# A hybrid decoder block on one core: the framework's scheduler orders all engines with its finer model of the machine

## The chip, the core and the metric

One core of a Trainium2 chip. The time is device microseconds of one execution, the median of several runs. The core's engines run side by side, each its own list of instructions in order: TensorE (PE, with its weight loads PEld), VectorE (DVE), ScalarE (ACT), GpSimd (POOL), and SyncE (SP), which issues most DMAs. Semaphores tie the lists together.

## The reference

x is 2048 x 1024 in f32, one layer.

```python
mod = cs @ ada_w + ada_b                        # sh1, sc1, g1, sh2, sc2, g2
h = rmsnorm(x, norm1_g) * (1 + sc1) + sh1
p = h @ w_in                                    # 3456 columns, shared out among three mixers
ya = rglru_mixer(...)                           # 256 wide: conv, gates, a linear scan over time
yb = hgrn2_mixer(...)                           # 384 wide: 6 heads, gated linear attention
yc = rwkv7_mixer(...)                           # 384 wide: 6 heads, a delta rule with state S per head
x = x + g1 * ((concat[ya, yb, yc] * mix_beta) @ w_out)
h = rmsnorm(x, norm2_g) * (1 + sc2) + sh2
x = x + g2 * ((silu(h @ w_gate) * (h @ w_up)) @ w_down)     # 2816 wide
out = rmsnorm(x, final_g)
```

rwkv7_mixer steps through time with `S = S * w + sa (kk a)^T + v k^T`, `y = S r`; the kernel does this in chunks of 64 steps.

## The kernel before

Time is cut into four blocks b = 0 to 3 of 512 columns, features lie on the 128 partitions.

*Dense products.* All of w_in, w_out, w_gate, w_up, w_down go through `project`. Each f32 operand is split into a high part in fp32r (ACT, line 78, `wh` or `hh`) and the remainder (DVE, line 221, `wl` or `hl`), and each 128 x 128 by 128 x 512 product is three matmuls at line 248, which add up in a PSUM bank `pd` (three of these):

```python
for n, (a, b) in enumerate(((wh, hh), (wh, hl), (wl, hh)), 3 * k):
    PE.matmul(p, a[:, c], b, start=(n == 0), stop=(n == tot - 1))
```

There are 9696 of them: 2592 for w_in, then per block 192 for w_out, 1056 up and 528 down, 1776 in all. A weight piece of 128 x 512 serves 12 matmuls per block; it is loaded by SP into one of three `wr` and split into one of four `wh`/`wl`.

*Mixers.* `mixers(b)` runs rwkv on three pairs of heads, hgrn on three pairs and rglru on two, on what w_in left in DRAM (`pd` there), and writes y to DRAM (`yd`). rwkv uses tiles `tr` and banks `pm`, `pc`; hgrn and rglru use `th` and the one bank `ph`. One rwkv pair goes so: low-rank projections (PE lines 488, 489), gates, a scan and decays (tables of ACT change several times), KG and BK (DVE 529 to 542), products within chunks (PE 553) masked on DVE (556, 557), transposes (562), the upper 32 x 32 blocks to DRAM (`nd`) and back over all partitions (`NL`, `NX`), a substitution of 30 x 2 short DVE operations (599, 601), back over DRAM (`xd`), transposes and two products (617 to 627), then the recurrence: eight chunks, each a chain PE 641, 642 - DVE 644 and ACT `rs` - PE 650 - DVE 651 and ACT `VS` - PE 653, 654 - DVE `VS` at line 81, and the next chunk begins from that state. A norm (257, 258: block sums), a gate (669) and the store end it. The three pairs of a block share tiles and follow one another, and the state ties block to block.

*What ties mixers and dense work.* w_out of block b needs all of its y: `load_y(b)` reads back `yd`, k = 0 to 7, where k = 5 to 7 are rwkv's pairs.

```python
def mixers(b):
    with level("mix"):
        lr = lora(b)
        rwkv(b, 0, lr); hgrn(b, 0); rglru(b, 0)
        rwkv(b, 1, lr); rwkv(b, 2, lr)
        hgrn(b, 1); rglru(b, 1); hgrn(b, 2)
...
    for b in range(NB):
        if b + 1 < NB:
            mixers(b + 1)
        with level("feed"):
            ys, before = ffn(b, *w_out_products(b, ys, before))
```

(Several lines of `mixers` stand on one here.)

*What sets the order.* The framework's scheduler takes the instructions as the program issues them, keeps a model of the machine running, and gives each engine, when the model says it can take one, the ready instruction with the lowest number. The numbers come from `level`:

```python
clock = {"out": -1000000, "load": 0, "feed": 1000000, "mix": 2000000, "dense": 3000000}
```

So mixers go before dense matmuls wherever the model has them ready. The lists that come out are fixed when the kernel is built.

## Time and profile before

| | |
|---|---|
| median of 3 runs | 2881.95 us (2878.94 to 2886.17) |
| the profiled execution | 2884.81 us |
| its span, first to last instruction | 2883.0 us |
| mean granted TensorE clock | 0.986 |
| instructions | 41762 |

In the profile's groups a line reads: line, engine, operation, output <- inputs, shapes, count | busy us, mean ns of one | idle time of the engine before them and what ended it. An f32 matmul of the mixers is recorded as two. Windows give, for each stretch, its length and the busy time of PE, PEld, DVE, ACT and POOL with counts, then granted clock, DMA share and GB/s.

### The profile page before, as it was taken

To read this page: it belongs to the slowest core of one execution; us is meant where nothing else is said; L and a number is where in the kernel's file an instruction comes from. 1 tells how busy PE (TensorE), PEld (TensorE's weight loads), DVE (VectorE), ACT (ScalarE), POOL (GpSimd) and SP (SyncE) were. 2 spreads that over 40 slices of the span, in tenths; PEclk is the share of its full clock that TensorE was granted. 3 is DMA by queue.
4 is the path that set the end of the run, shared out by engine and by line. 5 is a ranking of instruction groups with operands and counts; after the bars stand their busy time and mean duration, and the time that the engine had idled before them with its cause. 6 is when DMAs were issued, how large, how long until landed. Compare 5 with 4: busy or idle time off the path is not lost. (4 is left out here: it accounts for less than half of the span.)

```text
span 2883.0 us, 41762 instructions
## 1 busy us (share of the span) xinstructions
PE 2761.2 (96%) x14842; PEld 2189.4 (76%) x14842; DVE 1975.3 (69%) x4617; ACT 1500.2 (52%) x2514; POOL 81.5 (3%) x67
## 2 busy tenths in 40 slices
PE   7999999999999899999989999999999999999998
PEld 6777777777777677777767787777777888788886
DVE  8776768778586777868788777778964444644445
ACT  4528465263636737565684556757644233533323
POOL 2000000000001000000100000001000001000000
PEclk9999999999999999999999999999999999999999
DMA  7534455434344233333453233344432333433332
GB/s 255 161 103 142 137 160 182 129 121 133 98 125 142 89 88 100 103 92 100 115 160 88 84 105 101 96 114 122 122 94 88 96 99 117 146 99 96 98 96 87
DMA packets 235041, 337.52 MB, mean 117 GB/s; under 512 B 73041, under 2 KB 78673, under 8 KB 234833
## 3 DMA queue, kind: packets, MB, share of 16 engines
q1 hardware_dynamic: 160144, 285.55, 31.9%
q10 hardware_dynamic: 74688, 49.31, 6.7%
q8 instruction: 117, 1.92, 0.3%
q14 instruction: 92, 0.75, 0.1%
HBM read 286.53 MB, written 48.23 MB: 116 GB/s over the span
## 5 line engine op out<-in xcount | busy, mean ns | idle before, releaser
L248 PE MATMUL pd<-hh,wh 128*128 128x512 f32 x3232 | 1285.4, 399 | 16.6 <-ACT hh L78 14.2
L248 PE MATMUL pd<-hl,wh 128*128 128x512 f32 x3232 | 1289.3, 399 | 3.1 <-DVE hl L81 3.0
L248 PE MATMUL pd<-hh,wl 128*128 128x512 f32 x3232 | 1283.6, 397 | 0.0
L78 ACT ACTIVATE wh<-wr 128x512 fp32r<-128x512 f32 (+1 forms) x752 | 463.6, 620 | 865.3 <-PE pd L248 713.4
L221 DVE TENSOR_TENSOR wl<-wr,wh 128x512 fp32r<-128x512 f32 (+1 forms) x752 | 509.0, 681 | 315.6 <-ACT wh L78 307.7
L248 PEld LDWEIGHTS pd<-hh,wh 128*128 128x128 f32 x3232 | 611.3, 189 | 144.0 <-ACT hh L78 17.7
L248 PEld LDWEIGHTS pd<-hl,wh 128*128 128x128 f32 x3232 | 611.8, 189 | 129.1 <-DVE hl L81 7.4
L248 PEld LDWEIGHTS pd<-hh,wl 128*128 128x128 f32 x3232 | 611.9, 189 | 121.9 <-issue 2.6
L81 DVE SCALAR_TENSOR_TENSOR xs<-pd,Q,xs 128x512 f32<-128x512 f32 x224 | 167.6, 748 | 124.6 <-PE pd L248 114.5
L78 ACT ACT_TABLE_LOAD x183 | 234.8, 1283 | 12.1 <-issue 4.7
L78 ACT ACTIVATE xs<-pd 128x512 f32<-128x512 f32 x140 | 82.8, 591 | 66.0 <-PE pd L248 60.8
L78 ACT ACTIVATE th<-th 128x512 f32<-128x512 f32 (+2 forms) x153 | 93.7, 613 | 44.9 <-DVE th L787 19.7
L917 DVE TENSOR_TENSOR xs<-pd,xs 128x512 f32<-128x512 f32 x88 | 60.7, 690 | 77.0 <-PE pd L248 75.2
L78 ACT ACTIVATE hh<-xs 128x512 fp32r<-128x512 f32 x120 | 74.1, 627 | 38.1 <-DVE xs L917 25.3
L78 ACT ACTIVATE hw<-VS,we 64x64 f32<-64x64 f32 x192 | 66.0, 344 | 42.2 <-DVE VS L81 38.8
L599 DVE TENSOR_TENSOR ftmp<-NX,NL 128x30 f32<-128x30 f32 (+4 forms) x360 | 73.9, 205 | 8.6 <-issue 1.2
L601 DVE TENSOR_TENSOR NX<-NX,ftmp 128x30 f32<-128x30 f32 (+4 forms) x360 | 73.7, 205 | 7.2
L78 ACT ACTIVATE tr<-tr 128x512 f32<-128x512 f32 (+3 forms) x100 | 62.3, 626 | 16.8 <-DVE tr L81 15.0
L81 DVE SCALAR_TENSOR_TENSOR VS<-pc,we,hw 64x64 f32<-64x64 f32 x168 | 47.4, 282 | 32.7 <-PE pc L653 28.9
L217 POOL TENSOR_TENSOR hl<-xs,hh 128x512 fp32r<-128x512 f32 x32 | 46.8, 1488 | 810.4 <-ACT hh L78 571.3
L78 ACT ACTIVATE xs<-xs 128x512 f32<-128x512 f32 x77 | 47.7, 626 | 36.1 <-DVE xs L81 22.9
L221 DVE TENSOR_TENSOR hl<-xs,hh 128x512 fp32r<-128x512 f32 x88 | 61.8, 703 | 5.6 <-ACT hh L78 1.1
(234 smaller groups left out, 2665.1 us busy)
## 6 DMA issues: line engine op xcount, KB each, us to landing
wr<-in_w_gate SPq DMA_DIRECT2D x176, 256.0 KB, 2.6
wr<-in_w_upf SPq DMA_DIRECT2D x176, 256.0 KB, 2.6
wr<-in_w_down SPq DMA_DIRECT2D x160, 256.0 KB, 2.7
wr<-in_w_in SPq DMA_DIRECT2D x144, 256.0 KB, 3.3
pd<-xs SPq DMA_DIRECT2D x108, 256.0 KB, 2.9
xs<-in_x SPq DMA_DIRECT2D x72, 256.0 KB, 4.4
wr<-in_ada_w SPq DMA_DIRECT2D x64, 256.0 KB, 3.3
th<-pd ACTq DMA_DIRECT2D x64, 256.0 KB, 3.4
```

The costliest lines, as they stand in the source:

```text
L78: return A.activation(o, i, f, **k)
L81: return V.scalar_tensor_tensor(o, a, s, b, op0=op0, op1=op1)
L217: G.tensor_sub(lo, src, hi.bitcast(F))
L221: V.tensor_sub(lo, src, hi.bitcast(F))
L248: PE.matmul(p, a[:, c], b, start=(n == 0), stop=(n == tot - 1))
L599: V.tensor_mul(tv, NX[:, 0:m, j:j + 1].to_broadcast([128, m, n]), NL[:, j:j + 1, j + 1:32].to_broadcast([128, m, n]))
L601: V.tensor_add(NX[:, 0:m, j + 1:32], NX[:, 0:m, j + 1:32], tv)
L917: V.tensor_mul(t, pu, t)
```

## The change

One argument of the framework's context, so that the scheduler keeps a finer model of the machine while it places the instructions. Operations, tiles, buffers and priorities are the same; 183 ACT table loads at line 78 become 187, since they are put in by the order of the activations.

```diff
-    with tile.TileContext(nc) as tc:
+    with tile.TileContext(nc, schedule_with_timeline_sim=True) as tc:
```

All engines' lists differ. Three places follow; `pd`, `pm`, `pc`, `ph` are PSUM banks, other names as above.

TensorE, block 2, last rwkv pair, inside the recurrence, before (L732 is hgrn's):

```order
L653 MATMUL pc<-VS,BK 128x128
L654 MATMUL pm<-GIQ,VS 128x128
L732 MATMUL ph<-QZ,th 64x64 x6
L641 MATMUL pc<-VS,KG 128x128
L642 MATMUL pm<-KG,VS 128x128
L248 MATMUL pd<-hh,wl 128x512
L248 MATMUL pd<-hh,wh 128x512
L248 MATMUL pd<-hl,wh 128x512
L650 MATMUL pc<-rs,GIQ 128x64
```

The same pair now, from its first products to the recurrence:

```order
L248 MATMUL pd<-hh,wl 128x512
L553 MATMUL pm<-KG,BK 128x256 x8
L562 MATMUL pm<-C,BK 128x128 x8
L257 MATMUL pm<-tr,bones 128x512
L258 MATMUL pm<-tr,bones 128x512
L576 MATMUL pm<-C,tr 128x128 x4
L641 MATMUL pc<-VS,KG 128x128
L621 MATMUL pm<-tr,GIQ 32x32 x8
L626 MATMUL pm<-GIQ,tr 32x32 x8
```

The whole pair, 102 instructions, now stands between two dense matmuls, the 6165th and the next; before, it had dense matmuls between its own and was through 1182 dense matmuls earlier. Block 3's last pair stands likewise, 97 instructions behind dense matmul 7941.

DVE, the end of that pair's substitution, before:

```order
L601 TENSOR_TENSOR NX<-NX,ftmp 128x7x3
L81 SCALAR_TENSOR_TENSOR xs<-pd,Q_81,xs 128x512
L221 TENSOR_TENSOR wl<-wr,wh 128x512
L599 TENSOR_TENSOR ftmp<-NX,NL 128x16
L81 SCALAR_TENSOR_TENSOR VS_14599<-VS_14599,th,ph 64x64
L601 TENSOR_TENSOR NX<-NX,ftmp 128x8x2
```

And now:

```order
L601 TENSOR_TENSOR NX<-NX,ftmp 128x7x3
L599 TENSOR_TENSOR ftmp<-NX,NL 128x16
L601 TENSOR_TENSOR NX<-NX,ftmp 128x8x2
L606 MEMSET NX 32x8
L599 TENSOR_TENSOR ftmp<-NX,NL 128x8
L601 TENSOR_TENSOR NX<-NX,ftmp 128x8
```

No weight split (L221 `wl`) and no sum of a dense product (L81 `xs`) stands among these 60 rows any more.

TensorE, block 1, last rwkv pair, its first products, before:

```order
L248 MATMUL pd<-hh,wl 128x512
L553 MATMUL pm<-KG,BK 128x256 x6
L248 MATMUL pd<-hh,wh 128x512
L248 MATMUL pd<-hl,wh 128x512
L553 MATMUL pm<-KG,BK 128x256 x2
```

And now, where L257 and L258 on `ph` and L702 are hgrn's:

```order
L553 MATMUL pm<-KG,BK 128x256 x6
L257 MATMUL ph<-th,bones 128x512
L258 MATMUL ph<-th,bones 128x512
L553 MATMUL pm<-KG,BK 128x256 x2
L562 MATMUL pm<-C,BK 128x128 x8
L257 MATMUL pm<-tr,bones 128x512
L258 MATMUL pm<-tr,bones 128x512
L702 MATMUL ph<-C,th 128x128 x4
L576 MATMUL pm<-C,tr 128x128 x4
```

The rest of this pair, two hgrn pairs and one rglru, 343 instructions, stand between dense matmul 4389 and the next.

## The prediction

> **What bounds the kernel now.** I read the page's busy table, the windows by stage (all engines, then L248 alone), the chain, the waits, and at last the timeline of one step of the recurrence. From the page, the windows, the windows of L248 alone and the chain:
>
> ```profile
> span 2883.0 us, 41762 instructions
> PE 2761.2 (96%) x14842; PEld 2189.4 (76%) x14842; DVE 1975.3 (69%) x4617; ACT 1500.2 (52%) x2514; POOL 81.5 (3%) x67
> ...
> 2200.00:2300.00 100.00, 100.00 (x443) 82.84 (x442) 43.58 (x65) 31.28 (x51) 0.00 (x0) 1.00 0.34 101
> 0.00:2187.00 2187.00, 2083.14 (x11876) 1632.09 (x11877) 1653.68 (x4135) 1261.19 (x2129) 69.98 (x59) 0.99 0.41 121
> ...
> 0.00:2187.00 2187.00, 1725.35 (x6744) 1244.45 (x6745) 0.99 0.41 121
> sum 2883.00, PE 2398.27 PEld 1799.64; mean PE 1199.14 PEld 899.82
> ...
> 2186.90 271.55 PE pd L248 x1198
> ```
>
> TensorE is busy 96% of the span. With nothing but dense matmuls (2200 to 2300 us) it starts 443 in 100 us, 0.2257 us each, so the 9696 dense ones (L248, 3 x 3232) need 2188 us. L248 is shown busy for 2398 us, 210 us more than that. TensorE's other work is 2761 - 2398 = 363 us, its idle time 2883 - 2761 = 122 us. So 2883 = 2188 + 363 + 210 + 122, and the last two, 332 us, are loss. The mixers are done at 2187 us; from then on the chain is dense matmuls alone. The loss lies ahead of that: 6744 dense in 2187 us are 1522 us of work, shown as 1725.
>
> [...]
>
> **The change, part by part.** Nothing is added or removed but four ACT table loads (183 to 187 at L78, 4 x 1.283 us on an engine that is 52% busy: nothing on the path). All else is order, and engines run in order.
>
> *What moves.* In the old order TensorE gets the mixers' matmuls early: between two matmuls of rwkv's recurrence stand some 3 to 11 dense ones, and the last of block 3 stands at dense matmul 6742 of 9696, long ahead of the 7,920 where block 3's w_out first needs them. In the new one about 21 dense stand between any two of the recurrence's matmuls (my count of the rows in blocks 2 and 3), so 4.7 us pass between them, and a mixer block is finished only when the dense work has run out: block 1 at dense 4389, block 2 at 6165, block 3 at 7941, each 21 dense after the block's border (4368, 6144, 7920), which is k = 0 to 6 of the first w_out group, 7 x 3. The eighth k needs the last mixer output. There stand 343, 102 and 97 instructions on TensorE with almost no dense matmul between. I call these stretches A (rwkv pair 2 from L553, two hgrn, one rglru), B and C (all of rwkv pair 2). In them the mixers' chain, hidden under dense work so far, lies bare.
>
> Its price, from the rows by form:
>
> ```profile
> L78 ACT ACT_TABLE_LOAD x183 | 234.8, 1283 | 12.1 <-issue 4.7 <-DVE tr L81 3.1 <-PEq L1024 0.7
> L78 ACT ACTIVATE tr<-tr 128x512 f32<-128x512 f32 x48 | 30.1, 627 | 0.5
> L81 DVE SCALAR_TENSOR_TENSOR tr<-tr,P 128x512 f32<-128x512 f32 x52 | 38.5, 744 | 2.2 <-ACT tr L78 2.1
> L529 DVE TENSOR_TENSOR KG<-tr 64x512 f32<-64x512 f32 x24 | 16.4, 685 | 0.2
> L556 DVE TENSOR_TENSOR GIQ<-pm,C 64x256 f32<-64x256 f32 x96 | 39.8, 414 | 1.6 <-PE pm L553 1.5
> L557 DVE TENSOR_TENSOR KG<-pm,C 64x256 f32<-64x256 f32 x96 | 40.5, 422 | 1.9
> ```
>
> B, piece by piece. *Front*, from the last step of pair 1 to L553: ACT goes through 7 table loads (9.0 us) and 16 activations of about 0.63 us (10 us), with two detours over DVE and TensorE for block sums (2.3 us); then DVE has 14 operations of about 0.69 us (9.7 us): 31 us. *Masks* L556 and L557: 8 x (0.414 + 0.422) = 7 us. *Round trips over DRAM*, from the DMA view:
>
> ```profile
> nd<-GIQ ACTq DMA_DIRECT2D x48, 32.0 KB, 1.7
> NL<-nd ACTq DMA_DIRECT2D x48, 128.0 KB, 2.7
> xd<-NX ACTq DMA_DIRECT2D x48, 32.0 KB, 2.3
> GIQ<-xd ACTq DMA_DIRECT2D x48, 32.0 KB, 2.2
> yd<-tr ACTq DMA_DIRECT2D x12, 256.0 KB, 2.6
> xs<-yd SPq DMA_DIRECT2D x32, 256.0 KB, 3.9
> ```
>
> With 0.3 to 0.6 us for each of 4, 8, 4 and 4 issues the first trip takes 11 us and the second 8.5 us. *Substitution* between them and *one step* of the recurrence, from the timelines of DVE and of all engines:
>
> ```profile
> 2104.40 0.19 DVE L599 TENSOR_TENSOR ftmp<-NX,NL 128x29 f32<-128x29 f32 x1
> 2104.63 0.19 DVE L601 TENSOR_TENSOR NX<-NX,ftmp 128x29 f32<-128x29 f32 x1
> ...
> 2155.49 0.33 PE L650 MATMUL pc<-rs,GIQ 128*128 128x64 f32 x2
> 2155.86 0.22 DVE L651 COPY VS<-pc 64x64 f32<-64x64 f32 x1 [0.88 <-PE pc L650]
> 2156.11 0.22 ACT L78 ACTIVATE VS<-pc 64x64 f32<-64x64 f32 x1 [0.88 <-DVE VS L651]
> 2156.41 0.46 PE L653 MATMUL pc<-VS,BK 128*128 128x128 f32 x2
> 2156.91 0.60 DVE L81 SCALAR_TENSOR_TENSOR VS<-pc,we,hw 64x64 f32<-64x64 f32 x2 [0.83 <-PE pc L653]
> 2157.65 0.46 PE L641 MATMUL pc<-VS,KG 128*128 128x128 f32 x2
> 2158.86 0.21 DVE L644 COPY rs<-pc 64x64 f32<-64x64 f32 x1
> 2159.11 0.22 ACT L78 ACTIVATE rs<-pc 64x64 f32<-64x64 f32 x1 [0.65 <-DVE rs L644]
> 2159.57 0.33 PE L650 MATMUL pc<-rs,GIQ 128*128 128x64 f32 x2
> ```
>
> 60 x 0.23 = 14 us for the substitution, 5 us for the transposes and L621, L626. A step takes 4.08 us there; without the dense matmuls and DVE work that delay L644 by 0.7 us it is 3.4 us. In a bare stretch the clock counts too:
>
> ```profile
> 872.00:876.00 4.00, 0.32 (x2) 0.00 (x0) 1.29 (x2) 0.86 (x2) 0.00 (x0) 0.96 0.94 228
> 876.00:880.00 4.00, 3.23 (x23) 1.98 (x24) 1.26 (x9) 0.85 (x2) 1.27 (x1) 0.50 0.79 220
> 880.00:884.00 4.00, 4.00 (x51) 3.19 (x49) 2.09 (x11) 3.97 (x7) 1.98 (x2) 0.50 0.86 286
> ```
>
> After 4 us without matmuls the granted clock (third number from the end) is 0.50, still so 8 us later though TensorE is busy again. So I take half clock all through A, B and C, which adds about 0.5 us to a step: 8 x 3.9 = 31 us. *Tail*: statistics at the rates above 9 us, five DVE operations 3.5, the output to DRAM 2.6 and back as y 3.9, its split 1: 20 us. Sum of B: 31 + 7 + 11 + 14 + 8.5 + 5 + 31 + 20 = 128 us. C lacks the next block's lora work in its tail: 121 us.
>
> The Trainium skill (TensorE: Matmul & The Clock Gate, Part 1: The HAM clock gate) has the clock at half after an idle window of about 3.4 us and full again after about 3.4 us of sustained work. The fall agrees with the rows above; the return took longer there. By the page's figures a dense restart costs some 2 us three times, 6 us in all (an estimate).
>
> A: DVE has 321 instructions in that one gap, ACT 186. At their rows' means they are 125 us on DVE and 92 us on ACT; the larger ones beside those above:
>
> ```profile
> L81 DVE SCALAR_TENSOR_TENSOR VS<-VS,th,ph 64x64 f32<-64x64 f32 x168 | 46.9, 279 | 18.3 <-PE ph L777 14.3
> L740 DVE COPY_PREDICATED AQ<-M,ph 64x256 f32<-64x256 int8 x72 | 37.8, 525 | 4.3 <-PE ph L732 3.0
> L757 DVE TENSOR_TENSOR th<-th 128x256 f32<-128x256 f32 x72 | 29.9, 415 | 0.1
> ```
>
> DVE alone, 125 us, is the floor; DVE and ACT one after the other, 217 us, the ceiling. rwkv's part alone is B without its front, 97 us, and runs beside the hgrn chain; I take 165 us, below the middle, since two chains fill each other's gaps.
>
> Gross 165 + 128 + 121 = 414 us. TensorE does useful work in it: 542 of its 2811 listed mixer instructions, 19% of 363 = 70 us, and 8 dense, 2 us. Net +342 us. Bounds: DVE's busy time alone, counted in the same way (125 + 66 + 59), gives 250 - 72 = +178; all in series, with ACT's 92, 53 and 42 and 30 us of trips in B and C each (217 + 149 + 131), gives 497 - 72 = +425.
>
> *What is won back.* Elsewhere the order is kinder: a mixer matmul 21 dense after its predecessor waits for nobody, and the runs of mixer matmuls between dense ones fall from 679 to 462. The 210 us over 679 returns are 0.31 us each; 217 fewer save 67 us. Of the 122 us of idle time most stays: the start before the first matmul, the norm statistics at each block's border. I take 18 us, together -85. Bounds: 0, and 200 (60% of the 332).
>
> *Supply of dense work*: in the new DVE order a weight split (L221 wl) still stands every 6 or so rows among the substitution's; each serves 12 dense matmuls, 2.7 us, and four buffers cover the rows between. No cost.
>
> Sum: +342 - 85 = +257. On the profiled execution (2884.81 us, 1.8 over its span) that is 3142; it lies 0.1% above the median of 2881.95, so 3139 against the median.
>
> **The rivals.** *Faster*: the order wins back more than it lays bare. Place: the mixed phase; it decides once recovery exceeds the net exposure. For it speaks the pool of 332 us; against, that the exposure's floor is 178, so over 54% of the pool would have to go while its border waits and its start stay. At floor and a recovery of 250: 2882 - 72 = 2810. *Half*: chains run near DVE's floor and 120 us come back: 2882 + 178 - 120 = 2940, still slower. *Worse*: A runs in series (+52 over my 165), the half clock doubles the mixers' 70 us on the path (58 beyond the 12 in the steps) and nothing is recovered: 2882 + 342 + 52 + 58 = 3334 at most; 3260 with half of the recovery and of the clock's 58. For it speaks the clock of 0.50 while TensorE was busy; against, that the matmuls are a small part of a step.
>
> **How the numbers follow.** Forecast as told, 3020 to 3240: 0.80. Half, 2890 to 3020: 0.08. Worse, over 3240: 0.07. Faster: 0.03. Within 0.3% (what a measurement here can tell from no change): 0.02, where the two cancel. The range is the forecast's own: recovery 0 to 150 and exposures between +255 and +360 give 2990 to 3240, and the lowest corner is left out.
>
> **What would show it.** Right: three stretches of 100 to 190 us with next to no L248, ending near dense 4390, 6166 and 7942; granted clock 0.50 in them, its mean down from 0.986 to about 0.93; TensorE's busy share near 88%; the last L654 about 400 us before the end (1754 dense x 0.2257), not 700; between blocks fewer and shorter waits. Wrong: L248 going on through those stretches, stretches under 60 us, or an idle time that grows between them, which would mean that the new order makes TensorE wait for weights.

## The result, and the profile after

The changed kernel takes 3250.26 us (median of 4 runs, 3245.22 to 3254.75) against 2883.53 (2878.94 to 2886.17) on the same chip: a ratio of 1.127, interval 1.125 to 1.130. It is 367 us slower; the forecast was 3139, with 3020 to 3240 as its range, so the direction and the kind of loss were right and the size was 111 us short. The profiled execution took 3248.79 us.

The page of the changed kernel, in the rows that answer to those of before (span, busy times, and the granted TensorE clock in 40 slices):

```profile
span 3247.0 us, 41814 instructions
...
PE 2846.8 (88%) x14842; PEld 2284.8 (70%) x14842; DVE 1987.7 (61%) x4617; ACT 1511.6 (47%) x2518; POOL 81.4 (3%) x67
...
PEclk9999999999889999995589999957999996699999
```

TensorE's busy share has fallen from 96% to 88%, and the clock shows three deep dips, in slices 19 and 20, 27, and 34 and 35. They are the three stretches. A weaker one, in slices 11 and 12, lies about the end of w_in; on the page of before, all 40 slices show a 9. To see what they cost and what became of the rest, I cut both executions at the same places of the dense work: the start of dense matmul 2592 (the last of w_in), 4368, 6144 and 7920 (a block's border), and 28 matmuls behind each of these three borders. First the old order, by window (length; busy time and count of PE, PEld, DVE, ACT, POOL; clock):

```profile
0.00:871.93 871.93, 817.24 (x4685) 645.91 (x4686) 638.33 (x1637) 446.02 (x758) 23.13 (x23) 0.99 0.47 146
871.93:1442.40 570.47, 546.09 (x3124) 425.55 (x3123) 433.32 (x1085) 361.80 (x605) 27.82 (x22) 0.98 0.35 103
1442.40:1451.69 9.29, 9.29 (x44) 7.24 (x43) 8.42 (x16) 6.17 (x10) 0.00 (x0) 1.00 0.34 110
1451.69:1993.34 541.65, 523.71 (x2987) 410.50 (x2986) 424.73 (x1040) 339.02 (x567) 19.04 (x14) 0.99 0.37 107
1993.34:2001.66 8.32, 8.32 (x37) 6.38 (x36) 8.22 (x15) 5.14 (x8) 0.00 (x0) 1.00 0.37 104
2001.66:2453.52 451.86, 445.00 (x2179) 357.27 (x2178) 260.70 (x523) 196.07 (x335) 11.51 (x8) 0.99 0.36 106
2453.52:2461.31 7.79, 7.79 (x33) 5.93 (x32) 6.79 (x12) 4.34 (x7) 0.00 (x0) 1.00 0.33 93
2461.31:2883.00 421.69, 403.79 (x1760) 330.64 (x1758) 194.75 (x294) 141.69 (x227) 0.00 (x0) 0.98 0.34 104
```

And the new order, cut at the same dense matmuls:

```profile
0.00:864.14 864.14, 797.96 (x4467) 643.38 (x4468) 557.08 (x1355) 419.22 (x689) 21.76 (x21) 0.96 0.45 142
864.14:1433.44 569.30, 528.28 (x3055) 420.60 (x3054) 401.98 (x929) 341.10 (x552) 25.76 (x19) 0.95 0.35 101
1433.44:1611.69 178.25, 92.39 (x667) 69.90 (x665) 126.04 (x360) 102.59 (x168) 3.59 (x3) 0.59 0.16 45
1611.69:2087.89 476.20, 462.02 (x2338) 375.54 (x2337) 298.65 (x675) 219.05 (x374) 11.86 (x10) 0.97 0.35 104
2087.89:2228.90 141.01, 60.65 (x231) 41.35 (x230) 73.40 (x213) 61.38 (x106) 5.12 (x4) 0.57 0.13 35
2228.90:2683.70 454.80, 441.85 (x2106) 362.43 (x2104) 270.84 (x604) 180.81 (x320) 10.39 (x8) 0.98 0.36 104
2683.70:2823.69 139.99, 59.24 (x227) 40.12 (x226) 65.31 (x193) 46.44 (x86) 2.91 (x2) 0.56 0.10 27
2823.69:3247.00 423.31, 404.40 (x1760) 331.48 (x1758) 194.44 (x293) 140.97 (x226) 0.00 (x0) 0.98 0.34 103
```

The third, fifth and seventh rows are the 28 dense matmuls behind each border. They took 9.3 + 8.3 + 7.8 = 25.4 us and now take 178.3 + 141.0 + 140.0 = 459.3: 434 us more. These are A, B and C. The five other rows, the rest of the span, took 2857.6 us and now take 2787.8: 70 us less. Is that a gain? The matmul counts say no. In the border rows stood 114 records, now 1125, so 1011 mixer records have moved there. The mixers have 14842 - 9696 = 5146 records, and the forecast took 363 us of work for them, 0.0705 us each; so priced, 71 us of work moved. The rest of the program got shorter by what left it, and on balance by nothing else: 434 - 70 = 364 us net.

The balance hides two parts. A row's length less its busy time of PE is TensorE's idle time. In the five rows together it rose from 122 to 153 us, 28 of these 31 us ahead of the first border (54.7 to 66.2 and 24.4 to 41.0), where the clock has its weaker dip too; the busy time fell by 101 us. So busy time fell by 30 us more than the 71, and idle time took them back. If a mixer record costs more than 0.0705 us, which the price of a return below suggests, even these 30 us are mixer work that moved.

### The profile page after: what moved, and what is told of

Read it like the earlier page. It is cut to its first block, busy times and chain, and to the rows that moved or that the text cites. A ratio compares the mean times of both kernels' runs of the same rounds, so it can differ in the third digit from the quotient of the medians.

```text
span 3247.0 us, 41814 instructions
## 1 busy us (share of the span) xinstructions
PE 2846.8 (88%) x14842; PEld 2284.8 (70%) x14842; DVE 1987.7 (61%) x4617; ACT 1511.6 (47%) x2518; POOL 81.4 (3%) x67
## 4 chain that ended last, share of the span: by engine, by line
PE 63%; DVE 12%; ACT 12%; DMA 8%; issue 4%; ACTq 1%; SPq 0%; POOL 0%; DVEq 0%; POOLq 0%
PE pd L248 53%; ACT L78 4%; ACT tr L78 2%; DVE xs L81 2%; ACT th L78 2%; DMA xs<-in_x 1%; DMA tr<-pd 1%; DVE wl L221 1%; DMA wr<-in_w_in 1%; PE ph L732 1%; ACT wh L78 1%; DMA wr<-in_ada_w 1%; PE pc L653 1%; PE pm L553 1%; PE pc L641 1%
## 5 line engine op out<-in xcount | busy, mean ns | idle before, releaser
L248 PE MATMUL pd<-hh,wh 128*128 128x512 f32 x3232 | 1288.8, 402 | 58.0 <-ACT hh L78 43.8
L248 PE MATMUL pd<-hl,wh 128*128 128x512 f32 x3232 | 1292.5, 400 | 5.0 <-POOL hl L217 3.4
L248 PE MATMUL pd<-hh,wl 128*128 128x512 f32 x3232 | 1288.1, 399 | 4.2 <-DVE wl L221 4.2
L248 PEld LDWEIGHTS pd<-hh,wh 128*128 128x128 f32 x3232 | 617.9, 192 | 200.9 <-ACT hh L78 51.9
L221 DVE TENSOR_TENSOR wl<-wr,wh 128x512 fp32r<-128x512 f32 (+1 forms) x752 | 513.9, 685 | 357.5 <-ACT wh L78 347.0
L248 PEld LDWEIGHTS pd<-hl,wh 128*128 128x128 f32 x3232 | 618.2, 191 | 137.8 <-POOL hl L217 6.4
L248 PEld LDWEIGHTS pd<-hh,wl 128*128 128x128 f32 x3232 | 617.5, 191 | 134.5 <-DVE wl L221 7.3
L81 DVE SCALAR_TENSOR_TENSOR xs<-pd,Q,xs 128x512 f32<-128x512 f32 x224 | 167.6, 748 | 139.1 <-PE pd L248 130.3
L78 ACT ACTIVATE xs<-pd 128x512 f32<-128x512 f32 x140 | 82.8, 591 | 59.9 <-PE pd L248 32.3
L78 ACT ACTIVATE VS<-pc 64x64 f32<-64x64 f32 x96 | 20.9, 218 | 131.7 <-DVE VS L651 130.8
L81 DVE SCALAR_TENSOR_TENSOR VS<-pc,we,hw 64x64 f32<-64x64 f32 x168 | 47.4, 282 | 54.0 <-PE pc L653 51.2
L553 PE MATMUL pm<-KG,BK 128*128 128x256 f32 x192 | 54.1, 435 | 23.8 <-DVE BK L538 23.8
```

The costliest lines, as they stand in the source:

```text
L78: return A.activation(o, i, f, **k)
L81: return V.scalar_tensor_tensor(o, a, s, b, op0=op0, op1=op1)
L221: V.tensor_sub(lo, src, hi.bitcast(F))
L553: PE.matmul(ps[:, (c - q) * 256:(c - q + 1) * 256], BK[:, c, :], KG[:, c], start=True, stop=True)
```

## The experiments

**Theories.** *Laid bare*: a block's mixers need more dense matmuls between their own than a block has, so a remainder stands bare at each border, and the 364 us are that remainder. *Won back*: the forecast's 85 us exist and something in the stretches hides them. *Elsewhere, or only moved*: the new lists serve the dense work or the mixers' inputs badly all over.

**More dense work per product.** If a block had more dense matmuls, the chains would be covered. A fourth matmul per product does that. It leaves the mixers and the splits as they are; each split then serves 16 dense matmuls and not 12, so VectorE and ScalarE have more time for it too, and this run doesn't part the two:

```diff
-        tot = 3 * len(h)
+        tot = 4 * len(h)
...
-for n, (a, b) in enumerate(((wh, hh), (wh, hl), (wl, hh)), 3 * k):
+for n, (a, b) in enumerate(((wh, hh), (wh, hl), (wl, hh), (wl, hl)), 4 * k):
```

Old order:

> The old order, with a fourth dense matmul (wl, hl) in each product, so 12928 instead of 9696; nothing is left out. Control for the next run: 2883 + 3232 x 0.2257 = 3613 us, between 3590 and 3630.

New order:

> The new order, with the same fourth dense matmul. Order as built: an rwkv pair still takes some 850 dense matmuls from one end to the next, but a block now has 2368 of them and not 1776, so that the last pairs end at dense 4861, 7511 and 10242, ahead of the borders at 5824, 8192 and 10560, and no run of more than 40 mixer matmuls is left; runs of mixer matmuls are 577 against 642 with the old order. Theory 'laid bare, nothing won back' (the 367 us are the chains for which the dense work of a block is too short): as fast as the old order with four terms, within 1%, 3580 to 3650. Forecast's term 'won back' (85 us, 0.31 for each return to dense work spared and 18 of idle time): 20 us for 65 returns and up to 18 of idle time under the old order, and 60 to 85 under it if what comes back hangs on the wider spacing. Rival 'the new order serves the dense work badly': 100 us or more above the old order.

Measured: 3620.36 us with the old order (3619.53 to 3621.91) and 3605.65 with the new one (3604.04 to 3606.55). Against the kernel before these are 1.2568 (1.2549 to 1.2587) and 1.2515 (1.2494 to 1.2536). Of 367 us of loss nothing is left, and the new order is 15 us ahead, 0.4%. In the new order the 28 dense matmuls behind the three borders take 7.3, 6.9 and 6.6 us. The first lines of the two pages, the old order, then the new:

```profile
span 3618.6 us, 48231 instructions
```

```profile
span 3604.1 us, 48327 instructions
```

This shows two things. The loss hangs on the supply of dense work ahead of the borders, since the order was made in the same way and no stretch is left. And what the new order wins where it lays nothing bare is 15 us, not 85.

**The price of a return.** The forecast had put the 85 us down mostly to returns from mixer to dense matmuls, 0.31 us each. That price can be measured by itself, in a small kernel whose TensorE order is fixed (lines joined here; it ran once):

```diff
+    for _ in range(80):
+        mix(1); dense(10)
+    for _ in range(20):
+        mix(4); dense(40)
+    for d in (1, 3, 5, 8, 21):
+        dense(48); chain(48, d)
...
+    dense(48); chain(96, 0)
```

> A kernel of its own that measures the price of a return and of a chain link; it computes nothing of the reference. TensorE's order is fixed: dense matmuls (128x512, fp32r) alone; then 80 runs of one f32 matmul 128x128 with 10 dense behind each; then 20 runs of four with 40 dense behind each (both 80 f32 and 800 dense); then chains of 48 links (f32 matmul, VectorE reads its bank and writes the next link's operand) with 1, 3, 5, 8 and 21 dense between links; then 3 and 21 dense with a 128x512 VectorE operation ahead of each link's own; then 96 links with no dense. Forecast's 0.31 us for each return: the 80 runs take 60 x 0.31 = 18.6 us longer than the 20. 'A return is cheap' (0.09 us by the changed kernel's trace): 5 us longer or less. Chains, from the recurrence's step of three links in 3.4 us: a link alone 1.1 us, so 1 dense between leaves 0.7 us of wait, 3 leave 0.3, 5 and more none; a VectorE operation ahead adds about 0.6 at 3 dense and nothing at 21. If 21 dense were needed for a chain to wait for nobody, 5 and 8 would show waits. Clock in the bare chain: 0.50 to 0.60, and a link there 1.1 to 1.4 us.

Its windows: the 80 runs, the 20 runs, of the chains those with 1, 3 and 21 dense between links, and the one without any; then the 80 and the 20 runs again, with the dense matmuls alone (L59 there):

```profile
205.76:408.97 203.21, 203.21 (x962) 168.01 (x961) 0.00 (x0) 0.00 (x0) 0.00 (x0) 1.00 0.00 1
408.97:608.34 199.37, 199.37 (x961) 167.98 (x960) 0.00 (x0) 0.00 (x0) 0.00 (x0) 1.00 0.00 1
619.31:660.63 41.32, 34.34 (x145) 19.61 (x144) 13.66 (x47) 0.00 (x0) 0.00 (x0) 1.00 0.00 1
671.64:715.53 43.89, 43.89 (x241) 36.16 (x240) 13.97 (x48) 0.00 (x0) 0.00 (x0) 1.00 0.00 0
...
913.92:1155.40 241.48, 241.48 (x1105) 199.82 (x1104) 14.53 (x49) 0.00 (x0) 0.00 (x0) 1.00 0.00 1
1473.81:1584.29 110.48, 74.14 (x193) 46.78 (x192) 27.60 (x95) 0.00 (x0) 0.00 (x0) 0.52 0.00 0
...
205.76:408.97 203.21, 203.21 (x801) 144.32 (x800) 1.00 0.00 1
408.97:608.34 199.37, 186.43 (x801) 148.86 (x801) 1.00 0.00 1
```

Sixty returns more cost 203.21 - 199.37 = 3.8 us, 0.064 us each, a fifth of 0.31. Priced so, the 217 returns spared are 14 us, and the 65 spared with four terms 4 of the 15 us seen there; what the other 11 are is open.

The last two rows show where 0.31 came from. In the small kernel's first dense stage the matmuls start 0.2267 us apart, so 800 of them need 181 us. They are shown busy for 203 and 186 us: 22 us more over 80 returns, 5 over 20, so 0.25 to 0.27 us for each return, nearly the forecast's figure. But a return costs 0.064 us. The rest is the f32 matmuls' own work, which the records of the dense ones, with their modelled ends, cover. Such a matmul takes (199.4 - 181.4 - 1.3) / 80 = 0.21 us, 0.105 for each of its two records (an estimate for 128x128 alone), where 363 us over all mixer records give 0.0705. By this, part of the 210 us was mixer work, which no order can win back; how much, no run here shows.

The chains tell why wider spacing brings nothing: less its dense matmuls at 0.2267 us, a link costs 0.235 us with 3 dense between (43.89 / 48 - 0.68) and 0.271 with 21 (241.48 / 48 - 4.76). At three dense the wait is gone, and with one dense TensorE is idle for 7 of 41 us. The recurrence's links are longer, some 1.1 us (3.4 / 3) against 0.87 here at full clock, so three dense may fall a little short there; but in the kernel before, TensorE waited for the recurrence's three links for 12 us in the whole span (3.9 at L641, 3.3 at L650, 5.0 at L653). Its 3 to 11 dense left little to free, and 21 are no better. The stage with a VectorE operation ahead of each link's own came out as without it (43.9 us), since that operation waits for nobody and had run before; so it says nothing on a loaded VectorE; that case stands in the runs with four terms, where wider spacing meets a VectorE that is 55% busy, and the gain is 15 us.

**A shorter chain.** The substitution is left out in both orders:

```diff
-        for j in range(1, 31):
-            m, n = (j + 3) // 4, 31 - j
...
-            V.tensor_add(NX[:, 0:m, j + 1:32], NX[:, 0:m, j + 1:32], tv)
```

> The new order, with the substitution's 30 x 2 short VectorE operations (L599, L601) left out, so that the triangular inverse isn't computed; 14.6 us less in each pair's chain. Order as built: block 1's pairs now end at dense 4269, so A is gone; of B some seven recurrence steps and the tail are left, of C eight steps and the tail. 'Laid bare': B 7 x 4.0 + about 20 = 45 to 50 us, C 8 x 4.0 + 20 = 52 us, less some 10% of useful work, so 2883 + 85 = about 2970 us, between 2940 and 3000. Rival 'elsewhere' (the loss lies in how the new order serves the dense work, not in the chains): not more than the 3 x 14.6 = 44 us come off, 3200 or more.

> The old order, with the same 60 VectorE operations of each pair left out (12 x 14 us of VectorE work). 'Laid bare': the chain lies under dense work there, so next to nothing comes off: 2860 to 2885 us. Rival 'VectorE is scarce' (its work delays TensorE all over): a good part of 12 x 14 = 168 us comes off, under 2830.

Measured: 3013.23 us with the new order (1.0446, 1.0416 to 1.0476) and 2884.69 with the old one (1.0013, 0.9999 to 1.0026). The new order's three border stages:

```profile
1439.75:1459.79 20.04, 9.33 (x31) 5.84 (x30) 15.65 (x30) 17.18 (x24) 0.00 (x0) 0.78 0.37 115
1992.15:2046.56 54.41, 29.66 (x89) 19.72 (x88) 25.57 (x58) 35.18 (x63) 3.45 (x3) 0.58 0.15 46
2521.25:2586.58 65.33, 38.94 (x163) 26.66 (x162) 23.24 (x55) 23.52 (x54) 1.27 (x1) 0.59 0.09 26
```

Under the old order VectorE is busy for 114 us less (1861 against 1975), and the time doesn't show it. Under the new one the same cut is worth 237 us, over five times the 44 us that the operations themselves had in the stretches: a shorter chain lets pairs end earlier, so A went and B and C shrank to 54 and 65. That speaks against *elsewhere*, by which the time would have stayed at 3200 or more. I had expected 2970 and at most 3000. The three stages are 114 us over the old order's 25, where 85 had been counted for them, and the rest of the span is 13 us longer: here too nothing is won back.

**Fixing the recurrence's places.** Under the new order, dense matmuls of given number are made to wait in the list for given steps of the recurrence:

```diff
+    due = [(2592 + 592 * (p - 2) - 130 - 18 * (7 - i), p // 3, p % 3 * 8 + i) for p in range(3, 12) for i in range(8)]
...
+                        while due and due[0][0] <= count[0]:
+                            order(i, steps[due[0][1]][due[0][2]])
+                            due.pop(0)
```

> The new order, with one more rule of order: the eight recurrence steps (L650) of each rwkv pair of blocks 1 to 3 must stand on TensorE ahead of given dense matmuls, so that a pair ends every 592 dense and the last one about 130 ahead of the border at which w_out needs it. Nothing is left out. Theory 'laid bare' (the whole loss is the three stretches A, B, C, which cost 133 + 114 + 114 = 360 us net, and the new order wins nothing back elsewhere): no stretch is left, 3250 - 360 = 2890 us, between 2875 and 2910, clock above 0.97. Theory 'won back' (the 85 us of the forecast exist, but are hidden behind something in the stretches): 2800 to 2830. Rival 'only moved' (the finer order delays the mixers' inputs on VectorE and ScalarE, so a forced place on TensorE only turns the bare stretch into waits spread between the steps): 3100 or more, with L248 idle behind recurrence matmuls.

> The same rule for the three pairs of block 1 alone. Order as built: stretch A is gone, B and C stand as in the changed kernel (102 and 97 mixer matmuls in one run each). Nothing is left out. 'Laid bare': the stretches add up one by one, 3250 - 133 = 3117 us, between 3100 and 3130; B 141 and C 140 us long as before. 'Won back': below 3090. 'Only moved': 3200 or more. If what is freed in block 1 lets block 2 run earlier, B would shrink as well and the time would fall under 3100.

Measured: 3110.93 us for all three blocks (1.079, 1.0763 to 1.0817), 3203.66 for block 1 alone (1.1116, 1.109 to 1.1141). *Laid bare*, as I had put it, fails here: it said that with the stretches all of the loss goes, 2890 and 3117 us. Both times lie where *only moved* had put them (3100 or more, 3200 or more). With the rule for block 1 the stage between w_in and the border, and the border itself:

```profile
862.90:1527.06 664.16, 587.28 (x3463) 464.66 (x3462) 480.83 (x1181) 389.84 (x646) 28.52 (x21) 0.92 0.33 94
1527.06:1563.78 36.72, 21.71 (x93) 15.28 (x92) 28.13 (x61) 33.36 (x55) 1.42 (x1) 0.61 0.24 74
```

A has shrunk from 178 to 37 us, and the stage ahead of it has grown from 569 to 664, by 95: 59 us of busy time, with 408 more records, and 36 us of idle time. Three rows from the waits of TensorE with all three blocks fixed (L657, L648 and L628 are L650, L641 and L621 there; in the kernel before the same waits were 3.3, 3.9 and 4.1 us):

```profile
PE pc L657 <- ACT rs L78: 20.2, 28, 3.9
PE pc L648 <- DVE VS L81: 14.7, 19, 3.3
PE pm L628 <- DVE tr L624: 14.7, 7, 3.3
```

So part of the loss only moved, from bare stretches to waits at the recurrence. One reason could be that the rule names the steps alone and the other trips of a pair were pressed together ahead of the first step. The next rule names every trip, at the distance from the pair's end that it has in the old order (the last line stands behind L553; the block sum is 472 dense ahead of the end, L562 390, L621 150, L626 146, and so on):

```diff
+    def mark(b, pr, rel, i):
+        if b:
+            marks.setdefault(b, []).append((2592 + 1776 * (b - 1) + 592 * (pr + 1) - 150 - rel, i))
...
+            mark(b, pr, 404 - q, i)
```

> The new order with a rule for every round trip of an rwkv pair of blocks 1 to 3, not for L650 alone: each of its groups on TensorE (block sums, L553, L562, L621, L626, L641, L650, L653, L669) must stand ahead of the dense matmul at which it stands in the old order, counted from the pair's end; pairs end 592 dense apart, 150 ahead of the borders. Nothing is left out. As built, no run of more than 41 mixer matmuls is left there, and steps are 16 to 19 dense apart. Theory 'squeezed' (what the coarse rule left, 3111 against 2881, came from trips that it pressed together ahead of each fixed step): 2875 to 2920. Rival 'late inputs' (the lists of VectorE and ScalarE, made with the finer model, bring the mixers' inputs later than these places): 2980 or more, with L562, L621 or L650 waiting for VectorE or ScalarE.

And the same for blocks 2 and 3 alone (`if b > 1`):

> The new order with the fine rule of pace_fine for the pairs of blocks 2 and 3 alone; block 1 is left as the changed kernel has it. Nothing is left out. As built, A stays (343 mixer matmuls in one run), B and C are gone. In pace_fine TensorE lost 86 us more than under the old order while block 1's mixers were hurried (dense 2592 to 4368), but only 7 and 18 more in the two blocks behind. Theory 'late start' (block 1's mixers begin behind a backlog from the w_in part, which no rule reaches; where a block starts level, the new order holds the old one's pace): B and C come off, 114 + 114, and some 60 come back as shorter waits, 3250 - 170 = 3080 us, between 3050 and 3100. Rival 'late inputs everywhere' (any block hurried under the new order loses what block 1 lost in pace_fine, 86 us over the old order's figure): 3250 - 228 + 2 x 86 = about 3195, 3150 or more.

Measured: 3021.45 us (1.0487, 1.0448 to 1.0525) for blocks 1 to 3 and 3093.92 (1.0725, 1.0706 to 1.0745) for blocks 2 and 3. *Squeezed* had said 2875 to 2920 and fails as the whole account; the time lies where *late inputs* had put it, 2980 or more. From the first kernel the stage between w_in and the first border:

```profile
856.00:1527.99 671.99, 586.74 (x3467) 458.46 (x3466) 487.50 (x1198) 418.93 (x682) 31.68 (x22) 0.92 0.32 94
```

From the second kernel the stages ahead of the second and the third border:

```profile
1622.60:2168.35 545.75, 503.11 (x2537) 404.12 (x2535) 362.17 (x880) 280.78 (x478) 17.94 (x14) 0.94 0.34 98
...
2187.22:2673.02 485.80, 468.34 (x2277) 378.56 (x2275) 312.74 (x760) 224.57 (x400) 13.10 (x10) 0.98 0.36 104
```

Squeezing accounts for 90 of the 230 us that the coarse rule left. Of the 138 us left over the old order, the first stage holds some 77 (101.5 longer, less 24 for 343 more records); its idle time is 85 us where it was 24. There block 1's mixers start with a backlog: in the old order the first pair of block 1 had ended by dense 2267, in the new one block 0's last pair ends at 2544, and no rule reaches into w_in. With blocks 2 and 3 alone B and C go and the time falls by 156 us, where 170 were expected (3094 lies in the range of *late start*, 3050 to 3100); the stage ahead of the second border there is 36 us over the old order's and the one ahead of the third 27, each after its records are set off at 0.0705 us (545.75 - 541.65 with 450 fewer, 485.80 - 451.86 with 98 more). *Late start* fits best, but those 27 to 36 us a block stay unexplained: that VectorE's and ScalarE's lists bring the inputs late would fit, and no run here tells it apart. No such version comes near the kernel before.

**Less dense work.** If supply decides, the old order too must get stretches once a block's dense work is short:

```diff
-for n, (a, b) in enumerate(((wh, hh), (wh, hl), (wl, hh)), 3 * k):
+for n, (a, b) in enumerate(((wh, hh), (wh, hl)), 2 * k):
```

> The old order, with the third dense matmul of each product (wl, hh) left out, so 6464 instead of 9696 dense; the low part of the weights isn't multiplied. Theory 'supply' (a stretch lies bare wherever a block's dense work is shorter than its mixers' chain, in either order): a block now has 1184 dense, 267 us, less than its three pairs need, so the old order gets stretches too. As built, at each of the three borders some 380 mixer instructions stand among a dozen dense: the recurrence of pair 1 and all of pair 2, about 31 + 8 + 141 = 180 us. 2883 - 3232 x 0.2257 = 2154, plus 3 x 180 gross less 3 x 49 of useful work = about 2550 us, between 2450 and 2620. Rival 'the old order hides its chains whatever the supply': 2150 to 2200.

> The new order, with the same third dense matmul left out. As built: 546 mixer matmuls bare at block 1's border (about 250 us), 182 and 177 at the next two (about 190 us each), 317 at block 0's (about 200 us). 'Supply': 2154 + 830 - 152 of useful work = about 2830 us, between 2720 and 2930, so some 280 over the old order with two terms, nearly as much as the 367 with three. 'The new order is only slower to serve dense work': the gap to the old order shrinks with the dense work, to 245 us or less, with L248 idle outside the stretches.

Measured: 2678.83 us with the old order (0.9302, 0.9262 to 0.9343), 2887.07 with the new one (1.0017, 1.0000 to 1.0035). The old order's border stages:

```profile
1036.74:1247.48 210.74, 117.03 (x753) 83.59 (x752) 131.96 (x391) 108.45 (x202) 13.42 (x11) 0.60 0.18 49
1593.02:1807.20 214.18, 113.39 (x753) 81.78 (x751) 139.20 (x420) 112.41 (x206) 13.58 (x11) 0.62 0.18 50
2155.56:2365.79 210.23, 110.08 (x589) 79.09 (x588) 116.47 (x361) 95.90 (x175) 8.74 (x7) 0.56 0.16 43
```

The cut takes away 729 us of dense matmuls and only 205 us of time. The old order has stretches of some 212 us each, 32 longer than I had counted, which is 95 of the 129 us by which 2679 lies above 2550; the rest is open. Stretches are no property of the new order; they come where the chains need more cover than there is. The new order needs more of it: a pair takes some 850 dense matmuls there from end to end, some 560 in the old one, and a block offers 1184, 1776 or 2368 for three pairs. Three pairs at 850 are 2550, more than 2368 too. With four terms the new order is saved by the lead that the mixers win during w_in: the last pairs end 963, 681 and 318 dense ahead of their borders (5824 - 4861, 8192 - 7511, 10560 - 10242). The lead shrinks with each block, so more blocks would use it up; no run here has more. The gap between the orders is 208 us with two terms, 367 with three and -15 with four. With two, some 280 had been expected, and 245 or less was the rival's figure, by which the new order only serves dense work worse. It shrinks because the old order loses as well. Outside its three stretches the new order's TensorE is idle for 303 us, the old one's for 189; 98 of these 114 us lie between w_in's end and the first border, where a fourth stretch begins (from 700 to 820 us no L248 runs there). The chains account for most of it, and the rival isn't needed, but this run alone doesn't rule it out.

## Why the prediction was right and wrong

*What bounds the kernel, and where the loss arises.* Right. The three stretches came where the forecast put them, behind the three borders, with L248 all but absent. Windows of L248 alone (length, busy time and count of PE and PEld, clock):

```profile
1438.00:1613.00 175.00, 4.80 (x10) 1.97 (x8) 0.58 0.16 43
2088.00:2229.00 141.00, 11.06 (x30) 6.05 (x29) 0.57 0.13 35
2684.00:2824.00 140.00, 11.13 (x29) 6.11 (x28) 0.56 0.10 27
```

*Gross 165 + 128 + 121 = 414 us.* Measured 175, 141 and 140, 456 in these windows, which hold some 70 dense matmuls (16 us); 434 more than the old order's borders. The pieces of B can be read in its timeline; the rows are the wait for the substitution, the two ends of a step, the end of the recurrence and the first dense matmul behind it:

```profile
2160.00 1.03 PE L621 MATMUL pm<-tr,GIQ 32*32 32x32 f32 x16 [25.26 <-DVE tr L617]
...
2176.61 0.77 PE L641 MATMUL pc<-VS,KG 128*128 128x128 f32 x2 [0.36 <-DVE VS L81]
...
2180.76 0.77 PE L641 MATMUL pc<-VS,KG 128*128 128x128 f32 x2 [0.35 <-DVE VS L81]
...
2196.62 0.58 DVE L81 SCALAR_TENSOR_TENSOR Hc<-pc,we,hw 64x64 f32<-64x64 f32 x2 [1.14 <-PE pc L653]
...
2218.33 0.72 PE L248 MATMUL pd<-hh,wh 128*128 128x512 f32 x1
```

From 2091, where pair 1's recurrence ends, to that matmul pass 127 us: the sum had 128. TensorE waits 25 us for the substitution and the trips around it. A step takes 4.15 us (2176.61 to 2180.76) where 3.9 were taken, and from the recurrence's end to the first dense matmul behind it pass 21.7 us, where the tail was put at 20. What makes B's window longer lies behind that: the dense matmuls after the first wait once more, for splits and for the norm statistics, before the 28 are through. In A, VectorE was busy for 123 us and ScalarE for 102 (forecast 125 and 92).

*Half clock in the stretches.* Right: 0.56 to 0.58 there with their edges, 0.50 inside (below), and 0.912 over the span, where about 0.93 was told.

*Useful work, 72 us.* Right in the count of what moved: 71 us at the sum's own price for a record. That price is too low by the small kernel; at its 0.105 us the 1011 records would be 106 us (an estimate). The gross 434 less 70, by which the rest of the span shrank, leaves 364 us where the sum had +342.

*Won back, -85.* This is the step that failed. The sum took 217 returns at 0.31 us, 67 us, and 18 us of idle time. The idle time went the other way: outside the border rows it rose by 31 us. The forecast had named idle time that grows between the stretches as a sign of being wrong, and this is it, though waits for weights are 11.5 us of it at most. The returns cost 0.064 us each when measured, 14 us for 217, and at most 30 us of busy time can have come back. On balance it is nothing, and with four terms, where nothing is laid bare, it was 15 us in all. The price of 0.31 came from dividing all of L248's time beyond its work (210 us) by the number of returns (679), as if every one of those microseconds belonged to a return; the small kernel's records show as much for each return, and most of it is the f32 matmuls' own work. Nor did the wider spacing free the recurrence's matmuls from waiting: they had waited for 12 us in all. With 0 in place of -85 the sum is 2884.8 + 342 = 3227, inside the range; of the other 22 us, 20 are the stretches, whose gross was 434 us where 414 were taken. (That 342 + 22 gives the profiled 3249 is no test of its own, since 364 is the difference of the two spans.)

The Trainium skill (Perfetto Trace Analysis, Identifying the Most-Contended Engine) names the weight loads' busy share, beside MFU (the matmul work done as a share of the peak), in place of the matmul busy time as the measure of how much room TensorE has. In the kernel before, that share was 82.8% in dense work alone and 74.6% (1632 of 2187 us) ahead of 2187 us, which read as room is some 215 us (an estimate). The changed order used none of it, and with four terms the new order won 15 us: the share tells of room, not that another order finds it.

*Supply of dense work, no cost.* Nearly right. The groups of L248, in the changed kernel, then in the one before:

```profile
L248 PE MATMUL pd<-hh,wh 128*128 128x512 f32 x3232 | 1288.8, 402 | 58.0 <-ACT hh L78 43.8 <-ACT wh L78 7.3 <-DVE xs L81 4.4
L248 PE MATMUL pd<-hh,wl 128*128 128x512 f32 x3232 | 1288.1, 399 | 4.2 <-DVE wl L221 4.2
```

```profile
L248 PE MATMUL pd<-hh,wh 128*128 128x512 f32 x3232 | 1285.4, 399 | 16.6 <-ACT hh L78 14.2 <-ACT xs L78 2.4
L248 PE MATMUL pd<-hh,wl 128*128 128x512 f32 x3232 | 1283.6, 397 | 0.0
```

Waits for weights (`wh`, `wl`) grew from nothing to 11.5 us; the wait for `hh` grew by 30, the splits of inputs such as the last y at the ends of the stretches among them. *Between blocks fewer and shorter waits* was wrong for the stages but one: TensorE's idle time fell between the first and second border (17.9 to 14.2 us) and rose in w_in (54.7 to 66.2), ahead of the first border (24.4 to 41.0) and behind the second (6.9 to 13.0). *Last L654 about 400 us before the end*: 451, since C's tail and the program's last norm come on top of the dense work. The rivals *faster* and *half* rested on gains of the same kind, 250 and 120 us, and fall with them; *worse* (over 3240) holds the measured time and had one part right, nothing recovered, but its A in series did not come.

## What to carry to other kernels

When a scheduler's model of the machine changes, count in the new lists how much covering work stands between two dependent steps of the longest chain, multiply by the steps, and hold it against the covering work that there is ahead of the point where the result is needed: 12 pairs at some 850 dense matmuls, 10200, don't fit into the 7920 ahead of the last border, and 12 at 560 do. Before an unexplained remainder of busy time is divided by a count and called a price, measure that price in a kernel of a few hundred instructions; here it was a fifth, because the records of one kind of matmul covered the work of the other. And a wider spacing is worth something only up to the chain's own latency, which three dense matmuls covered in the small kernel; the waits at the chain's links tell whether anything is left to free.

## What the runs showed of the hardware

In the small kernel the bare chain, a matmul shown busy for 0.49 us in every 0.87, did not hold the clock. It never leaves TensorE idle for longer than 0.39 us, and yet the clock fell about 5 us after the chain began, stayed there for 105 us, and came back about 4 us after dense work set in at 1584.3. Windows at the fall and at the return:

```profile
1478.00:1480.00 2.00, 1.28 (x4) 0.80 (x4) 0.53 (x3) 0.00 (x0) 0.00 (x0) 0.74 0.00 0
1480.00:1482.00 2.00, 1.51 (x4) 1.00 (x4) 0.35 (x2) 0.00 (x0) 0.00 (x0) 0.50 0.00 0
...
1587.00:1588.00 1.00, 1.00 (x4) 0.81 (x3) 0.00 (x0) 0.00 (x0) 0.00 (x0) 0.50 0.00 0
1588.00:1590.00 2.00, 2.00 (x10) 1.64 (x9) 0.00 (x0) 0.00 (x0) 0.00 (x0) 0.96 0.00 0
```

With one dense matmul between links (busy 34 of 41 us) it held 1.00. So the clock was lost at a busy share of 56% (0.49 of 0.87 us) and held at 83%; whether the share or the length of the idles decides, no run here tells. The price: a link takes 110.48 / 96 = 1.15 us in the bare chain, nearly all of it at 0.50, and 41.32 / 48 = 0.86 with that one dense matmul in it at full clock; the matmul more is free, and the link is a quarter shorter.

The Trainium skill (TensorE: Matmul & The Clock Gate, Part 1: The HAM clock gate) ties the half clock to an idle window and the return to sustained work, both of some 3.4 us. It also tells of a kernel in which short idles between groups of matmuls made the clock swing, without a figure for them. The return agrees (about 4 us); the fall came here with idles of 0.39 us at most.

The changed kernel shows the same in B's recurrence, though longer waits stand ahead of it: from 2165 to 2196 us no idle time of TensorE is over 0.56 us, it is busy for 23.1 of 31 us, and the clock stays at 0.50 throughout.
